# Low parts of streamed weights: from a VectorE subtraction to a ScalarE negation and an adding transfer

## The chip, the cores and the metric

The kernel runs on one core of one Trainium2 chip. The metric is the device time of one launch in microseconds (us). The engines are TensorE (PE, its weight loads shown as PEld), VectorE (DVE), ScalarE (ACT), GpSimd (POOL) and SyncE (SP), which here issues DMA transfers.

## The reference

Two transformer-like networks run one after the other on 512 tokens of width 1024, all in float32. The first is one layer: a modulated norm, one projection `w_in` to queries, keys, values, gates and a recurrent branch, dilated attention in three groups, a gated linear recurrence, and the merge of both branches:

```python
mod = jax.nn.silu(c) @ w_mod + b_mod
h = rms_norm(x, g_pre) * (1 + scale) + shift
q, k, v, g_att, u, g_lru, merge = jnp.split(h @ w_in, split_at, axis=-1)
y_a = (dilated_attention(q, k, v) * jax.nn.silu(g_att)) @ w_pa
y_b = (rg_lru(causal_depthwise_conv(u, conv_w, conv_b), ...) * jax.nn.silu(g_lru)) @ w_pb
out = (gate_a * y_a + gate_b * y_b) @ w_o
x = x + gate * rms_norm(out, g_post)
```

The second is two layers over the 512 tokens and 256 context tokens. Each has four token mixers (a long convolution, differential attention over both streams, spatial gating, a short convolution) that share the projection `w_in_2` (ten parts of 256 columns) and `w_out_2`, and an MLP with a squared relu and 4096 hidden units. The context stream goes through the first layer's mixers and MLP, and in the second layer only through the keys and values.

## The kernel before

Activations lie transposed, 128 channels on the partitions by 512 (or 256) tokens, so a product is a sum over eight such tiles. To keep float32 accuracy with the faster fp32r format, each operand is held as a high part (the value rounded to fp32r) and a low part (the value less its high part), and `mm3` issues three matmuls for each product: high by high (L157), high weight by low activation (L158), low weight by high activation (L159). `tok3` (L164 to L166) does the same with the operands' places exchanged.

Weights stand in DRAM as blocks of 128 x 2048 floats. `whalf` (L141) makes one half of a block, 128 x 1024 or 512 KB: SP loads it into a `raw` buffer (four of them, RAW_BUFS; the load has its priority raised by 4000), ACT copies it to fp32r as `whi` (L149), and DVE subtracts `whi` from `raw` into `wlo` (L150). There are three buffers of `whi` and three of `wlo` (W_BUFS); L149 and L150 have their priority raised by HPS = 400. `whalf` is called 312 times: 8 times for `w_u`, the first projection, and 304 times for all others. `raw_half` with another pool loads the modulation weights (`rawa`), which DVE alone reads (L263); no `whalf` is in that.

`wblock` makes both halves of a block. `gemm` works through a block for its two output tiles and each stream of tokens; for each it passes over half 0 and then half 1, in four k-steps of three matmuls each, into one PSUM tile:

```python
todo = [(mi, st) for mi in range(2) for st in streams]
for grp in ([todo] if together else [[t] for t in todo]):
    pss_ = [ps.g() for _ in grp]
    for h, (hi, lo) in enumerate(halves):
        ...
```

The stages in order: `w_u` (to 66 us), four heads of attention with `w_head`, recurrence and `w_gl` (to about 450 us), the merge with `w_merge`, `w_pb`, `w_pa` (where a block of `w_pa` is loaded for two rounds, so one of its halves is held through the three blocks of the second round) and `w_o`, then for each layer of the second network the input projections (`in`), attention with the short convolution and most of `out_part` between its units, and the MLP (`up`, `down`; layer 0 from 1010 to about 1590 us with part of the context's work at its end, layer 1 from 1807 us). The context's projections of layer 0 (Mixer `mc`) have 256 columns only, and its `out_part("cdab")` holds halves of three blocks at a time.

No order is written out by hand between engines: the program is traced in the order of the source, and when it is built a scheduler fixes each engine's order from priorities and from the times at which it expects operands to be ready. On the chip an engine runs its list strictly in that order and waits where an operand is late. GpSimd's list holds little: 24 `pow` (L225) of the norms, each between a DVE operation and the transposes that spread its result.

Of the kernel before, what the change touches and what calls it, by code (L numbers as in the profile page):

```python
# [10 lines left out]
F32 = mybir.dt.float32  # L11
F32R = mybir.dt.float32r
BF16 = mybir.dt.bfloat16
AF = mybir.ActivationFunctionType
ALU = mybir.AluOpType
# [13 lines left out]
BLOCKS = {}  # L29
# [50 lines left out]
def tile_net(ctx: ExitStack, tc: tile.TileContext, wst, vec, crow, lrow, sgw, cst, xT, xN, cT, out):  # L80
    nc = tc.nc
    V, A, G, T = nc.vector, nc.scalar, nc.gpsimd, nc.tensor
# [3 lines left out]
    def nm(s):  # L86
        uid[0] += 1
        return f"{s}_{uid[0]}"
# [45 lines left out]
    def raw_half(key, h, pool=None):  # L134
        if pool is None:
            t = wpool.tile([P, 1024], F32, tag="raw", name=nm("raw"), bufs=RAW_BUFS)
        else:
            t = pool.tile([P, 1024], F32, tag="rawa", name=nm("rawa"), bufs=rawa_bufs[0])
        with tc.high_priority(offset=HP):
            nc.sync.dma_start(t, wst[BLOCKS[key]][:, h * 1024:(h + 1) * 1024])  # L140
        return t  # L141

    def whalf(key, h, cols):

        hi = wpool.tile([P, 1024], F32R, tag="whi", name=nm("whi"), bufs=W_BUFS)
        lo = wpool.tile([P, 1024], F32R, tag="wlo", name=nm("wlo"), bufs=W_BUFS)
        src = raw_half(key, h)
        with tc.high_priority(offset=HPS):
            A.copy(hi, src)  # L149
            V.tensor_sub(lo, src, hi.bitcast(F32))  # L150
        return hi.rearrange("p (k c) -> p k c", c=cols), lo.rearrange("p (k c) -> p k c", c=cols)

    def wblock(key, kt, cols):
        return [whalf(key, h, cols) for h in range(2)]
# [178 lines left out]
    for m in range(NT):  # L333
        mod_col(m, 1)
        mod_col(m, 0)
        hi, lo = whalf(("w_u", m // 2), m % 2, 1024)
        V.scalar_tensor_tensor(x0[m], x0[m], sc1[:, m:m + 1], pb0 if m else pbp, op0=ALU.mult, op1=ALU.mult)
        A.activation(h1[m][:, 0], x0[m], AF.Identity, bias=sh1[:, m:m + 1])  # L338
        V.scalar_tensor_tensor(h1[m][:, 1], x0[m], sh1[:, m:m + 1], h1[m][:, 0].bitcast(F32),
                               op0=ALU.add, op1=ALU.subtract)  # L340
        for c in range(NT):
            mm3(pu[c], hi[:, 0, c * P:(c + 1) * P], lo[:, 0, c * P:(c + 1) * P], h1[m][:, 0], h1[m][:, 1],
                m == 0, m == NT - 1)
        if m == 3:
            with tc.high_priority(offset=HP):
                nc.sync.dma_start(vecs, vec[:, NV0:NV])
    rawa_bufs[0] = RAWA_BUFS

# [39 lines left out]
    for mp in range(4):  # L388
        u = yap.tile([P, 2, SX], F32, tag="ya", name=nm("u"), bufs=4)
        for i in range(2):  # L390
            m = 2 * mp + i
            dst, src = u[:, i].rearrange("p (i r) -> p r i", r=4), pu[m].rearrange("p (r i) -> p r i", r=4)
# [415 lines left out]
    class Mixer:  # L808
# [334 lines left out]
        def out_part(self, names, done=None, bank=None):  # L1143

            s = self.s
            key = f"out{self.l}"
            for half in range(2):
                w = {n: whalf((key, 2 + half), "ab".index(n), 512) for n in names if n in "ab"}
                for pair in range(2):
                    if "c" in names:  # L1150
                        w["cd"] = whalf((key, half), pair, 256)
                    for i in range(2):
                        p = (bank or ps.g)()[:, :s.n]
                        seq = []
                        if "c" in names:
                            seq += [(w["cd"], kk, i, self.y["cd"[kk // 2], kk % 2]) for kk in range(4)]
                        for n in "ab":
                            if n in names:
                                seq += [(w[n], kk, 2 * pair + i, self.y[n, kk]) for kk in range(2)]
                        for e, ((hi, lo), kk, mi, a) in enumerate(seq):  # L1160
                            c = slice(mi * P, (mi + 1) * P)
                            mm3(p, hi[:, kk, c], lo[:, kk, c], a[:, 0], a[:, 1], e == 0, e == len(seq) - 1)
                        self.add(4 * half + 2 * pair + i, p, done)
# [177 lines left out]


RAW_BUFS = 4
RAWA_BUFS = 4
W_BUFS = 3
ST_BUFS = 2
# [158 lines left out]
```

## Time and profile before

| | us |
|---|---|
| median of 3 runs (lowest, highest) | 2175.99 (2171.11, 2178.37) |
| the profiled execution, its own time | 2175.18 |
| its span from the first to the last instruction | 2173.3 |
| PE busy | 2053.4 |
| DVE busy | 1424.4 |
| ACT busy | 810.1 |
| POOL busy | 27.4 |

Times in the rows are counted from the span's start. A matmul's busy time overlaps the next one's: starts of matmuls, not their durations, tell the pace. The granted clock (PEclk) is 1.00 at 2.4 GHz and 0.50 at 1.2 GHz; its mean over the span is 0.978. A bracket at a row's end is the engine's idle time before it and what ended it.

### The profile page before, as it was taken

What the parts mean: (1) busy time and instruction counts of PE and PEld (TensorE: products, weight loads), DVE (VectorE), ACT (ScalarE), POOL (GpSimd) and SP (SyncE); (2) the same over time, 40 slices, a digit from 0 to 9 for tenths busy, and PEclk for the clock granted to TensorE, in tenths of its full rate; (3) what the DMA queues carried; (4) which work ended last, traced back from release to release, by engine and by line L of the source; (5) the groups of instructions that cost most, each with busy time, mean ns of one, the idle gap of its engine ahead of it and who ended that gap; (6) DMA issues with size and microseconds to landing.
All of it is one profiled execution on the core that took longest, in us unless ns stands there. A gap on an engine that the chain in (4) does not pass through costs nothing.

```text
span 2173.3 us, 28000 instructions
## 1 busy us (share of the span) xinstructions
PE 2053.4 (94%) x11020; PEld 1758.3 (81%) x11020; DVE 1424.4 (66%) x2351; ACT 810.1 (37%) x1266; POOL 27.4 (1%) x28
## 2 busy tenths in 40 slices
PE   7989999999999988998999999999998998999997
PEld 5778788778889777876888888888887787888886
DVE  8778999843458999778354645534798766443444
ACT  3565333432344533645312313123434544232331
POOL 0000000000000000000000000000000000000000
PEclk9999999999999999998999999999999998999998
DMA  8523666523335444222232454422413212333331
GB/s 314 171 92 95 197 222 204 181 94 105 109 111 168 124 121 127 78 78 79 67 127 88 138 169 150 155 67 89 135 59 107 83 59 69 97 97 97 97 97 58
DMA packets 84388, 259.47 MB, mean 119 GB/s; under 512 B 11424, under 2 KB 20256, under 8 KB 84256
## 3 DMA queue, kind: packets, MB, share of 16 engines
q1 hardware_dynamic: 84256, 257.67, 37.6%
q8 instruction: 87, 1.43, 0.3%
q14 instruction: 45, 0.37, 0.1%
HBM read 242.95 MB, written 5.24 MB: 114 GB/s over the span
## 4 chain that ended last, share of the span: by engine, by line
PE 72%; DVE 18%; DMA 3%; issue 3%; ACT 3%; POOL 1%; SPq 0%; POOLq 0%; DVEq 0%; ACTq 0%
PE mm L157 15%; PE mm L159 15%; PE mm L158 15%; PE g L157 5%; PE g L158 5%; PE g L159 5%; DVE wlo L150 3%; DVE ya L872 2%; PE po L1084 2%; DVE rawa L263 2%; DVE j L263 1%; PE sc L1057 1%; DMA rawa<-wst 1%; PE mm L1081 1%; PE mm L208 1%
## 5 line engine op out<-in xcount | busy, mean ns | idle before, releaser
L149 ACT CAST whi<-raw 128x1024 fp32r<-128x1024 f32 x312 | 326.9, 1050 | 536.7 <-PE mm L158 387.4
L150 DVE TENSOR_TENSOR wlo<-raw,whi 128x1024 fp32r<-128x1024 f32 x312 | 380.5, 1222 | 210.7 <-ACT whi L149 205.9
L157 PE MATMUL mm<-h,whi 128*128 128x512 f32 (+1 forms) x992 | 361.0, 366 | 5.7 <-ACT h L338 3.6
L158 PE MATMUL mm<-h,whi 128*128 128x512 f32 (+1 forms) x992 | 361.7, 365 | 0.9 <-DVE h L712 0.9
L159 PE MATMUL mm<-h,wlo 128*128 128x512 f32 (+1 forms) x992 | 361.1, 364 | 0.8 <-DVE wlo L150 0.8
L159 PE MATMUL mm<-hid,wlo 128*128 128x512 f32 (+1 forms) x768 | 272.6, 355 | 1.0 <-DVE wlo L150 1.0
L157 PE MATMUL mm<-hid,whi 128*128 128x512 f32 (+1 forms) x768 | 273.0, 355 | 0.0
L158 PE MATMUL mm<-hid,whi 128*128 128x512 f32 (+1 forms) x768 | 272.8, 355 | 0.0
L157 PEld LDWEIGHTS mm<-h,whi 128*128 128x128 f32 x992 | 188.8, 191 | 37.1 <-ACT h L338 4.0
L158 PEld LDWEIGHTS mm<-h,whi 128*128 128x128 f32 x992 | 188.7, 190 | 31.5 <-DVE h L712 1.9
L157 PE MATMUL g<-h,whi 128*128 128x512 f32 x512 | 205.7, 402 | 8.6 <-DVE v L508 6.0
L159 PEld LDWEIGHTS mm<-h,wlo 128*128 128x128 f32 x992 | 188.6, 190 | 31.2 <-DVE wlo L150 2.0
L158 PE MATMUL g<-h,whi 128*128 128x512 f32 x512 | 204.8, 400 | 0.0
L159 PE MATMUL g<-h,wlo 128*128 128x512 f32 x512 | 204.3, 399 | 0.3 <-DVE wlo L150 0.3
L159 PEld LDWEIGHTS mm<-hid,wlo 128*128 128x128 f32 x768 | 146.1, 190 | 21.5 <-DVE wlo L150 1.4
L157 PEld LDWEIGHTS mm<-hid,whi 128*128 128x128 f32 x768 | 146.4, 191 | 20.2
L158 PEld LDWEIGHTS mm<-hid,whi 128*128 128x128 f32 x768 | 146.3, 191 | 20.0
L1284 DVE SCALAR_TENSOR_TENSOR r<-mm,r 128x512 f32<-128x512 f32 x96 | 57.4, 599 | 114.1 <-ACT r L1283 114.0
L157 PEld LDWEIGHTS g<-h,whi 128*128 128x128 f32 x512 | 98.4, 192 | 26.9 <-issue 6.2
L159 PEld LDWEIGHTS g<-h,wlo 128*128 128x128 f32 x512 | 98.1, 192 | 19.3 <-DVE wlo L150 0.7
L158 PEld LDWEIGHTS g<-h,whi 128*128 128x128 f32 x512 | 98.3, 192 | 17.9
L872 DVE SCALAR_TENSOR_TENSOR ya<-glu,caw,ya 128x512 f32<-128x512 f32 (+1 forms) x180 | 111.6, 656 | 0.5
(309 smaller groups left out, 3462.7 us busy)
## 6 DMA issues: line engine op xcount, KB each, us to landing
raw<-wst SPq DMA_DIRECT2D x312, 512.0 KB, 3.9
rawa<-wst SPq DMA_DIRECT2D x120, 512.0 KB, 4.6
qst<-q SPq DMA_DIRECT2D x48, 64.0 KB, 2.0
kst<-k SPq DMA_DIRECT2D x48, 64.0 KB, 2.0
kst<-k SPq DMA_DIRECT2D x72, 32.0 KB, 2.1
x<-xT SPq DMA_DIRECT2D x4, 512.0 KB, 5.0
hs_d<-c SPq DMA_DIRECT2D x4, 512.0 KB, 2.6
hq<-hs_d SPq DMA_DIRECT2D x4, 512.0 KB, 5.5
```

The source lines that it names most:

```text
L149: A.copy(hi, src)
L150: V.tensor_sub(lo, src, hi.bitcast(F32))
L157: T.matmul(ps, lh, rh, start=start, stop=False)
L158: T.matmul(ps, lh, rl, start=False, stop=False)
L159: T.matmul(ps, ll, rh, start=False, stop=stop)
L208: T.matmul(pt[:, i:i + 1], a[:, i * P:(i + 1) * P], ones1, start=k == 0 and i == 0, stop=k == len(self.parts) - 1 and i == nt - 1, skip_gr ...
L263: V.tensor_tensor_reduce(o, w, row, 0.5, 0.0, ALU.mult, ALU.add, d)
L872: V.scalar_tensor_tensor(self.ya[m], x, w, self.ya[m], op0=ALU.mult, op1=ALU.add)
L1057: T.matmul(st[:, o:e], hd.q[:, w, qt * P:(qt + 1) * P], hd.k[:, w, o - w * nkeys:e - w * nkeys], start=True, stop=True, skip_group_check=True)
L1081: T.transpose(pt[:, i * P:(i + 1) * P], pw[0][:, t0 + i * P:t0 + (i + 1) * P], ident)
L1084: T.matmul(hd.po[:, qt, h % 2], pth[:, i * P:(i + 1) * P], ss.v[:, kt, h], start=i == 0 and qt == 0 and h % 2 == 0, stop=i == nk - 1 and q ...
L1284: V.scalar_tensor_tensor(r, p, 0.0, r, op0=ALU.max, op1=ALU.mult)
```

## The change

For all blocks but `w_u` the subtraction goes. ACT writes the negative of the high part into `wlo`, and a transfer issued by GpSimd adds the raw weights to it from SBUF to SBUF, 512 KB each. The transfer stands under the same raised priority. `raw` is now read by ACT's copy and by the transfer; matmuls on `wlo` wait for the transfer to have landed.

```diff
         with tc.high_priority(offset=HPS):
             A.copy(hi, src)
-            V.tensor_sub(lo, src, hi.bitcast(F32))
+            if key[0] in LO_DMA:
+                A.activation(lo, hi.bitcast(F32), AF.Copy, scale=-1.0)
+                G.dma_start(lo.bitcast(F32), src, accum_op=ALU.add)
+            else:
+                V.tensor_sub(lo, src, hi.bitcast(F32))
@@
 RAW_BUFS = 4
+LO_DMA = tuple({k for k, _ in BLOCKS} - {"w_u"})
```

## Rows read from the trace of the kernel before

**Rows 1.** The page's part 1: busy us, share of the span, instructions.
```profile
PE 2053.4 (94%) x11020; PEld 1758.3 (81%) x11020; DVE 1424.4 (66%) x2351; ACT 810.1 (37%) x1266; POOL 27.4 (1%) x28
```

**Rows 2.** Busy time by stretch: three with a full DVE, and the second MLP.
```profile
core 0: us, PE busy (x) PEld busy (x) DVE busy (x) ACT busy (x) POOL busy (x), PEclk, DMA share, GB/s
163.00:434.70 271.70, 257.57 (x1474) 220.32 (x1473) 251.47 (x475) 103.35 (x170) 0.00 (x0) 0.99 0.56 180
652.00:869.30 217.30, 193.56 (x1264) 175.63 (x1263) 198.62 (x387) 90.81 (x160) 6.62 (x7) 0.95 0.45 135
1575.60:1684.30 108.70, 99.28 (x594) 87.55 (x593) 98.77 (x171) 41.91 (x71) 3.16 (x3) 0.95 0.29 83
...
1820.00:2160.00 340.00, 339.81 (x1504) 281.44 (x1502) 144.66 (x163) 104.89 (x132) 0.00 (x0) 1.00 0.29 89
```

**Rows 3.** PE's waits: line, releaser, us in total, times, longest.
```profile
PE mm L208 <- DVE acc L221: 17.6, 3, 10.4
...
PE g L159 <- DVE wlo L150: 2.4, 4, 0.9
...
PE mm L159 <- DVE wlo L150: 1.7, 4, 1.0
```

**Rows 4.** Timeline (start, us, engine, line, operation) in the second MLP.
```profile
1884.15 1.05 ACT L149 CAST whi<-raw 128x1024 fp32r<-128x1024 f32 x1 [7.11 <-PE mm L158]
...
1885.24 1.23 DVE L150 TENSOR_TENSOR wlo<-raw,whi 128x1024 fp32r<-128x1024 f32 x1 [2.87 <-ACT whi L149]
...
1890.03 0.39 PE L159 MATMUL mm<-hid,wlo 128*128 128x512 f32 x1
```

**Rows 5.** Timeline in the first MLP, both streams.
```profile
1110.32 1.05 ACT L149 CAST whi<-raw 128x1024 fp32r<-128x1024 f32 x1 [11.55 <-PE mm L158]
...
1114.84 0.39 PE L159 MATMUL mm<-hid,wlo 128*128 128x512 f32 x1
```

**Rows 6.** Timeline in the merge, with a half of w_pa held.
```profile
485.71 1.05 ACT L149 CAST whi<-raw 128x1024 fp32r<-128x1024 f32 x1 [1.94 <-PE mm L158]
...
488.89 0.40 PE L159 MATMUL mm<-yb,wlo 128*128 128x512 f32 x1
```

**Rows 7.** Timeline of PE: matmuls of other tiles between a tile's own.
```profile
169.58 0.42 PE L158 MATMUL big<-us,g 128*128 128x512 f32 x1
...
1594.13 0.40 PE L157 MATMUL g<-h,whi 128*128 128x512 f32 x1
1594.36 0.39 PE L158 MATMUL g<-h,whi 128*128 128x512 f32 x1
1594.59 0.28 PE L157 MATMUL g<-hc,whi 128*128 128x256 f32 x1
1594.71 0.40 PE L159 MATMUL g<-h,wlo 128*128 128x512 f32 x1
...
1818.60 0.39 PE L157 MATMUL mm<-h,whi 128*128 128x512 f32 x1
```

**Rows 8.** Groups of instructions: count, busy us, mean ns, idle before and releasers.
```profile
L150 DVE TENSOR_TENSOR wlo<-raw,whi 128x1024 fp32r<-128x1024 f32 x312 | 380.5, 1222 | 210.7 <-ACT whi L149 205.9 <-PE g L159 1.8 <-PE g L158 0.4
...
L149 ACT CAST whi<-raw 128x1024 fp32r<-128x1024 f32 x312 | 326.9, 1050 | 536.7 <-PE mm L158 387.4 <-PE g L158 92.9 <-issue 29.3
...
L225 POOL TENSOR_TENSOR rs<-ms,neghalf 128x4 f32<-128x4 f32 (+2 forms) x24 | 27.1, 1131 | 2135.4 <-DVE ms L233 1832.5 <-DVE ms L1099 161.4 <-DVE ms L929 136.9
```

**Rows 9.** DMA issues: count, KB each, median us from issue to landing.
```profile
raw<-wst SPq DMA_DIRECT2D x312, 512.0 KB, 3.9
...
qst<-q SPq DMA_DIRECT2D x48, 64.0 KB, 2.0
...
hs_d<-c SPq DMA_DIRECT2D x4, 512.0 KB, 2.6
```

**Rows 10.** Timeline of PE in the context's out_part.
```profile
813.95 0.58 PE L159 MATMUL g<-y,wlo 128*128 128x256 f32 x1 [0.90 <-DVE wlo L150]
```

**Rows 11.** A stop of PE, and the stretch behind it (columns as in rows 2).
```profile
858.39 0.55 PE L157 MATMUL mm<-sgs,sv 128*128 128x256 f32 x1 [3.91 <-DVE sb L951]
...
857.90:864.60 6.70, 6.21 (x19) 5.27 (x20) 6.56 (x8) 0.62 (x1) 0.00 (x0) 0.50 0.37 116
```

## The prediction

> **What bounds the kernel now.** I read the page's busy times first [rows 1]: TensorE (PE) is busy 2053.4 of 2173.3 us, so all its idle time is 119.9 us, and nothing done on another engine can give back more. VectorE (DVE) has 1424.4 us, ScalarE (ACT) 810.1, GpSimd (POOL) 27.4. Next the stretches [rows 2]: in the second layer's MLP PE is busy 339.81 of 340 us and DVE less than half, so there PE alone bounds. In the first block's attention, 163 to 435 us, DVE is busy 251.47 of 271.7 us and PE 257.57: DVE is almost as full, but PE stands only 14.1 us. Last the waits of PE [rows 3]: on the low parts of mm3 (L159) it loses 2.4 + 1.7 us in the whole run; the longest in total, 17.6 us, is for a norm's sum of squares, and most of the others are for such chains, which hold no weight work. So the kernel is bound by PE's stream of matmuls, and the weights arrive in time for it. The question is whether they still do.
>
> **How much time a low part has.** A block is two halves; gemm goes over them as half 0, half 1 for its first output tile and again for the second. With W_BUFS = 3 the next block's half 0 is ready early, but its half 1 goes into the buffer that the running block's half 0 leaves late in the block. One such cycle with 512 tokens [rows 4]: the buffer is left and the CAST starts at 1884.15, the subtraction ends at 1886.47, and the first matmul on that low part runs at 1890.03. That is 5.88 us from release to need, 2.3 of them used. In the first layer's MLP, where each block also serves 256 context tokens, the last pass over half 0 is a context pass, so the release comes later: 1110.32 to 1114.84, 4.52 us [rows 5]. While a w_pa half is held one buffer is missing and half 0 itself is late: 485.71 to 488.89, 3.18 us [rows 6]. For blocks with context alone I work it out: matmuls of 256 columns follow each other every 0.12 us [rows 7], a pass over a half has 12, so 1.44 us, and release to need is two passes and two matmuls, 3.1 us.
>
> **The change part by part.** (1) It takes 304 subtractions of 1222 ns off DVE (312 less the 8 of w_u): 371 us [rows 8]. (2) It adds 304 negations to ACT. An ACT pass over 128x1024 is the CAST, 1050 ns [rows 8]; 304 x 1.05 = 319 us, ACT then has 1129 of 2173, no bound, though its evacuations stand up to 1.05 us behind each one; PSUM banks cover that. (3) It adds 304 transfers of 512 KB on GpSimd's queue. In that queue stand the 24 pow of the norms [rows 8]; one may stand behind a transfer that waits for its negation. At one CAST each that is 24 x 1.05 = 25 us at most and nothing at least; I take 5. (4) Raw buffers are left when the transfer has landed instead of after the subtraction. With four of them a load still starts two blocks ahead; I take nothing for it, and name the price of full DMA engines in the first rival.
>
> After the change the chain to a low part is CAST 1.05, negation 1.05, two hops of 0.04 (as between CAST and subtraction [rows 4]), then the transfer, D from issue to landing: 2.18 + D, where it was 2.3. The trace shows no adding transfer and none issued by GpSimd. Its nearest rows [rows 9]: 512 KB out of the SBUF land in 2.6 us (plain, one read), a raw load of the same size takes 3.9, 64 KB take 2.0. From 64 to 512 KB a load costs 1.9 us, so a second read of the whole tile, which an addition needs, about 2.2. The low end of D is 2.6 (the second read hidden), the high end 3.9 + 2.2 = 6.1, and 8.3 if a raw load shares the engines. An estimate from these is 2.6 + 2.2 + an issue of 0.33 = 5.1; I take 5.0, so a chain of 7.2 us.
>
> The Trainium skill says, in "Collectives: The Full Stack", section "The bandwidth ceiling: the fold count and why AG ≠ RS ≠ AR", that an add in a DMA engine runs at half the rate of a copy because it reads two sources. No run here shows that yet. "DMA: Bandwidth & Descriptors", section "Anatomy of one DMA — SWDGE (gpsimd) path", fits a GpSimd transfer as 2.0 us plus bytes over 436 GB/s: 3.2 us for 512 KB; with the read doubled 4.4. Put into the sum below, the first would give about 2221 us (and the third rival's time with a fully adapted order), the second about 2283.
>
> If PE keeps its present order, each block stands for 2.18 + D less the time it has:
> - 60 blocks with 512 tokens outside the attentions (32 in the second MLP, 4 in the first, 12 of the input projections, 12 of the merge and w_o stage): 7.18 - 5.88 = 1.3 us each, 78 us.
> - 29 blocks with both streams (27 in the first MLP, 2 key and value blocks): 7.18 - 4.52 = 2.7, 78 us.
> - 6 blocks with a w_pa half held: 4.0, 24 us.
> - 14 blocks with context alone (10 of in0, 4 of down0): 4.1, 57 us.
> - The context's out_part, which holds all three buffers and already waits for low parts [rows 10]: four changes of weights at D less 0.1, 20 us.
> The w_head, w_gatt, first w_gl, short() and x out_part blocks stand between attention work that PE can do meanwhile: nothing; without that cover 30 blocks would cost 1.3 each, 39 us. Sum 257 us.
>
> But PE's order is made by the build, and the trace shows that it puts other matmuls in where a low part was expected late: at 1594.13 the two L157 and L158 matmuls of g<-h are followed by one of g<-hc, and only then by the L159 that needs the low part. There are 27 places where the instruction after such a pair is not its L159, the first at 169.58 and the last at 1818.60 us [rows 7]. A block taken as half 0, 0, 1, 1 has 10.9 us (one stream), 16.6 (both) or 6.0 (context) from release to need, and 5.9 with a buffer held. Then nothing is left for the first two kinds, 14 x 1.2 = 17 and 6 x 1.3 = 8, with out_part 20: 45 us. How late the build expects an adding transfer no row shows. I take the middle of 45 and 257, 151 us.
>
> What DVE gives back: PE's idle time in the stretches where DVE is over 80% busy is some 47 us (14.1 in 163 to 435, 23.7 in 652 to 869, 9.4 in 1576 to 1684 us [rows 2]). Much of it is chains without a subtraction in them, so I take 20 (bounds 0 and 47). The clock: after the 3.9 us stop at 854 us the granted clock was 0.50 for 6.7 us [rows 11], a loss of some 3.4 us. Of the stops above, 24 are of 4 us and more in the present order; half as long in the middle case, I take 4 falls, 14 us (bounds 0 and 24 x 3.4 = 82).
>
> Sum: +151 - 20 + 14 + 5 = +150 on the profiled execution's 2175.18 us (span 2173.3 and 1.9 around it; the median of the three runs, 2175.99, is 0.8 above): **2325 us**.
>
> **Rivals.** First, slow transfers in the present order: D near 6.5, the order not adapted. Each of the 113 places above then stands 1.5 us longer, 257 + 170 = 427, clock +40, DVE -20: about 2625. For it: the raw loads of the second MLP already take 0.29 of the DMA engines [rows 2], and as many bytes again, read twice, would bring them to about 0.9, where transfers queue. Against it: the order does adapt in the trace. Second, the order adapts fully: 45 - 20 + 5 = +30, 2205 (2185 to 2240). For it: the 27 places. Against it: it must expect at least the D that the chip shows. Third, faster: a D of at most 3.6 fits into the 3.7 us that a 512-token block leaves after the negation, and with an adapted order into the others; then only out_part pays 4 x 3 = 12 and DVE's relief decides: with 30 us of it 2157. The point from which it decides is D = 3.6; plain rows lie on both sides of it (2.6 and 3.9). Fourth, relief and waits cancel, or the low part is hidden everywhere and DVE's relief is worth nothing because PE's stream bounds: 2170 to 2182.
>
> **How the numbers follow.** Forecast (2240 to 2480) 0.50, slow transfers 0.12, full adaptation 0.18, faster 0.13, no change 0.07. Differences within 0.3% (6.5 us) can't be told from none here. So faster 0.13, same 0.07, slower 0.80. The range from 2172 to 2570 leaves out the faster case and the upper end of the slow one. Inside it the forecast's own range is 2240 to 2480.
>
> **What would show it.** Right: waits of PE for DMA on wlo at the head of the half-1 passes of the MLP, 1 to 3 us each, on the order of 100 of them; landing times of the adding transfers of 4.5 to 6 us; DVE near 1055 us and ACT near 1130; DMA share in the second MLP from 0.29 to 0.6 or above. PE busy near 100% in the MLP with L157 and L158 of two tiles alternating would show that the order adapted, and the second or third rival. Landings under 3.6 us would make the prediction wrong on its first term; landings over 6, low by the first rival. A wait of POOL's pow for ACT would show the queue's price; pow rows that begin as soon as now show it at nothing.

## The result, and the profile after

The changed kernel takes 2465.87 us (median of 4 runs, 2462.22 to 2483.36) where the kernel before takes 2175.09 beside it: 1.1354 times as long, with a 95% interval of 1.1296 to 1.1411. The forecast was 2325 us, so the sign was right and the loss of 291 us about twice the 150 forecast. The profiled execution took 2462.22 us, its span is 2460.4, or 287.1 us longer than before; the mean granted clock of PE fell from 0.978 to 0.954. Lines of the gemm stand four lower now: the three matmuls of a low-part product, L157 to L159 before, are L161 to L163, the CAST is still L149, the negation L151, the transfer L152. L169 is `tok3`'s matmul on a low part (L165 before).

From the page of the changed kernel: engines (busy us, share, instructions), queues, the group of the transfers, and landing times (count, KB, median us).

```profile
PE 2133.3 (87%) x11020; PEld 1793.3 (73%) x11020; DVE 1093.0 (44%) x2047; ACT 1103.4 (45%) x1570; POOL 289.1 (12%) x332
...
q0 software_dynamic: 43776, 159.40, 35.8%
...
L152 POOL DMA_DIRECT2D wlo<-raw x304 | 263.5, 867 | 2014.7 <-ACT wlo L151 1786.5
...
raw<-wst SPq DMA_DIRECT2D x312, 512.0 KB, 4.7
...
wlo<-raw POOLq DMA_DIRECT2D x304, 512.0 KB, 5.3
...
qst<-q SPq DMA_DIRECT2D x48, 64.0 KB, 4.1
```

Against [rows 1] DVE is relieved by 331 us and ACT loaded by 293, as meant, and both are under half full. PE does the same 11020 matmuls and is busy 79.9 us longer; its idle time went from 119.9 to 2460.4 - 2133.3 = 327.1 us, 207.2 more. These two make the 287.1. The waits of PE (line, releaser, us in total, times, longest) tell where the second comes from:

```profile
PE mm L163 <- DMA wlo<-raw: 120.3, 81, 4.3
...
PE g L163 <- DMA wlo<-raw: 79.5, 36, 12.2
...
PE mm L245 <- DVE rb L242: 15.0, 10, 2.2
...
PE g L169 <- DMA wlo<-raw: 13.4, 8, 4.1
```

Low parts cost PE 120.3 + 79.5 + 13.4 = 213.2 us, where it was 2.4 + 1.7 in [rows 3] and 0.9 in one wait of L165, 5.0 together: 208.2 more. All other idle time of PE was 114.9 us and is 113.9, so of DVE's 331 us of relief 1 us is left in the sum. (The row for rb is PE's wait for a norm's row, which comes behind GpSimd's pow.)

One cycle of the second MLP in the timeline (start, us, engine, line, operation, in brackets the idle time before and what ended it), to be laid beside [rows 4]:

```profile
2099.75 1.05 ACT L149 CAST whi<-raw 128x1024 fp32r<-128x1024 f32 x1 [0.52 <-PE mm L162]
...
2100.84 1.06 ACT L151 ACTIVATE wlo<-whi 128x1024 fp32r<-128x1024 f32 x1
...
2102.25 0.87 POOL L152 DMA_DIRECT2D wlo<-raw  x1 [8.23 <-ACT wlo L151]
...
2105.22 0.39 PE L161 MATMUL mm<-h,whi 128*128 128x512 f32 x1
...
2105.45 0.39 PE L162 MATMUL mm<-h,whi 128*128 128x512 f32 x1
...
2106.86 0.50 PE L163 MATMUL mm<-h,wlo 128*128 128x512 f32 x1 [1.02 <-DMA wlo<-raw]
```

The buffer comes free at 2099.75 and the low part is used at 2106.86: 7.11 us for the chain, where 5.88 were to be had. Of the 7.11, 4.6 run from the issue of the transfer to its landing, and 0.35 from the end of the negation to the issue. PE stands 1.02 us for it, and its first matmul after the stop takes 0.50 instead of 0.39. By stretch (columns as in rows 2): the attention stage of the first block, a piece around the context's out_part, and the second MLP.

```profile
67.50:510.00 442.50, 376.91 (x1969) 317.22 (x1968) 273.08 (x521) 216.83 (x314) 42.54 (x50) 0.93 0.74 201
...
922.60:984.20 61.60, 32.77 (x203) 29.98 (x203) 18.61 (x34) 17.50 (x20) 6.97 (x8) 0.75 0.75 186
...
2054.20:2445.50 391.30, 359.05 (x1535) 286.88 (x1536) 80.97 (x115) 171.41 (x200) 52.63 (x61) 1.00 0.70 162
```

The same stages in the kernel before, first and third of these:

```profile
66.40:449.20 382.80, 356.25 (x1969) 303.14 (x1968) 324.62 (x574) 168.30 (x263) 0.00 (x0) 0.98 0.50 162
...
1807.90:2158.60 350.70, 350.65 (x1535) 290.04 (x1536) 153.88 (x176) 110.45 (x139) 0.00 (x0) 0.99 0.28 86
```

The second MLP became 40.6 us longer: 32.2 us of idle time and 8.4 of busy time, at a granted clock of 1.00. The attention stage became 59.7 us longer. By the first matmul of each stage in the timelines the whole loss divides like this (us; "present order" is the prediction's sum without an adapted order, divided by stage from its own list):

| stage | present order | after |
|---|---|---|
| w_u, before the first attention | 0 | 1 |
| first block's attention (w_head, w_gatt, w_gl) | 0 | 59.7 |
| merge | 34 | 29.3 |
| w_o | 5 | 3.5 |
| context's in0 and out_part, input projections up to the first MLP | 69 | 61.4 |
| first MLP and the projections up to the second block | 108 | 93 |
| second block's attention | 0 | -1.7 |
| second MLP | 42 | 40.6 |

The last column holds the clock too: the trace has 13 stretches at half clock with 99 us together before, 43 with 227 us after. Half of that is lost at most, 64 us more; counting only the time in which PE is busy there, 68 and 169 us, an estimate is 51. The longest single wait for a low part, 12.2 us, is in the context's out_part: three transfers issued within 1.9 us of each other, from 944.04 us on, land 5.0, 6.8 and 9.7 us after their issue, and PE waits for the last. There the load counts, and not the chain alone.

### The profile page after: what moved, and what is told of

It is laid out like the page before. It is cut to its first block, busy times and chain, and to the rows that moved or that the text cites. A ratio compares the mean times of both kernels' runs of the same rounds, so it can differ in the third digit from the quotient of the medians.

```text
span 2460.4 us, 28758 instructions
## 1 busy us (share of the span) xinstructions
PE 2133.3 (87%) x11020; PEld 1793.3 (73%) x11020; DVE 1093.0 (44%) x2047; ACT 1103.4 (45%) x1570; POOL 289.1 (12%) x332
## 4 chain that ended last, share of the span: by engine, by line
issue 39%; PE 13%; POOL 4%; DMA 3%; DVE 1%; ACT 1%; POOLq 0%; DVEq 0%; ACTq 0%
POOL wlo L152 4%; DMA wlo<-raw 3%; PE g L163 2%; PE g L161 2%; PE g L162 2%; PE po L1088 2%; PE sc L1061 1%; PE mm L163 1%; PE mm L1085 1%; PE mm L161 1%; PE mm L162 1%; POOL rs L229 1%; PE mm L212 0%; PE g L169 0%; DVE sm L1065 0%
## 5 line engine op out<-in xcount | busy, mean ns | idle before, releaser
L149 ACT CAST whi<-raw 128x1024 fp32r<-128x1024 f32 x312 | 326.7, 1048 | 532.8 <-PE mm L162 374.0
L152 POOL DMA_DIRECT2D wlo<-raw x304 | 263.5, 867 | 2014.7 <-ACT wlo L151 1786.5
L163 PE MATMUL mm<-h,wlo 128*128 128x512 f32 (+1 forms) x992 | 368.7, 372 | 63.0 <-DMA wlo<-raw 62.8
L161 PE MATMUL mm<-h,whi 128*128 128x512 f32 (+1 forms) x992 | 364.5, 369 | 5.6 <-ACT h L342 3.6
L162 PE MATMUL mm<-h,whi 128*128 128x512 f32 (+1 forms) x992 | 364.6, 368 | 0.9 <-DVE h L716 0.9
L163 PE MATMUL mm<-hid,wlo 128*128 128x512 f32 (+1 forms) x768 | 280.1, 365 | 50.4 <-DMA wlo<-raw 50.4
L151 ACT ACTIVATE wlo<-whi 128x1024 fp32r<-128x1024 f32 x304 | 320.8, 1056 | 4.6
L161 PE MATMUL mm<-hid,whi 128*128 128x512 f32 (+1 forms) x768 | 276.3, 360 | 0.0
L162 PE MATMUL mm<-hid,whi 128*128 128x512 f32 (+1 forms) x768 | 275.9, 360 | 0.0
L163 PEld LDWEIGHTS mm<-h,wlo 128*128 128x128 f32 x992 | 190.7, 192 | 106.7 <-DMA wlo<-raw 78.1
L163 PE MATMUL g<-h,wlo 128*128 128x512 f32 x512 | 212.4, 415 | 33.1 <-DMA wlo<-raw 33.1
L161 PEld LDWEIGHTS mm<-h,whi 128*128 128x128 f32 x992 | 191.0, 193 | 37.1 <-ACT h L342 4.0
L161 PE MATMUL g<-h,whi 128*128 128x512 f32 x512 | 211.1, 412 | 5.2 <-ACT whi L149 3.2
L162 PEld LDWEIGHTS mm<-h,whi 128*128 128x128 f32 x992 | 190.6, 192 | 33.7 <-DVE h L716 2.2
L162 PE MATMUL g<-h,whi 128*128 128x512 f32 x512 | 210.1, 410 | 0.0
L163 PEld LDWEIGHTS mm<-hid,wlo 128*128 128x128 f32 x768 | 148.9, 194 | 81.4 <-DMA wlo<-raw 61.8
L162 PEld LDWEIGHTS mm<-hid,whi 128*128 128x128 f32 x768 | 149.0, 194 | 21.5
L161 PEld LDWEIGHTS mm<-hid,whi 128*128 128x128 f32 x768 | 149.2, 194 | 20.2
L1302 DVE SCALAR_TENSOR_TENSOR x<-mm,der,x 128x512 f32<-128x512 f32 x64 | 48.0, 751 | 246.6 <-PE mm L163 246.6
L163 PEld LDWEIGHTS g<-h,wlo 128*128 128x128 f32 x512 | 101.1, 198 | 60.0 <-DMA wlo<-raw 41.3
L1287 ACT ACTIVATE r<-mm 128x512 f32<-128x512 f32 x96 | 50.2, 522 | 197.7 <-PE mm L163 197.5
```

The costliest lines, as they stand in the source:

```text
L151: A.activation(lo, hi.bitcast(F32), AF.Copy, scale=-1.0)
L152: G.dma_start(lo.bitcast(F32), src, accum_op=ALU.add)
L161: T.matmul(ps, lh, rh, start=start, stop=False)
L162: T.matmul(ps, lh, rl, start=False, stop=False)
L163: T.matmul(ps, ll, rh, start=False, stop=stop)
L1287: A.activation(r, p, AF.Relu)
```

## The experiments

The theory after the first look was: what costs is the length of the chain CAST, negation, transfer, against the time between the release of a buffer and its use. The rivals: the DMA engines or GpSimd's queue are too full (load); ACT's added pass; the build's changed order of PE.

**The negation without the transfer.** The addition goes back to DVE; ACT's negation stays.

```diff
-                G.dma_start(lo.bitcast(F32), src, accum_op=ALU.add)
+                V.tensor_add(lo, lo.bitcast(F32), src)
```

> The ScalarE half of the change alone: the negation stays, but VectorE adds raw to it, so nothing goes over GpSimd or the DMA engines. Theory (the transfer's latency against the time between a buffer's release and its need is what costs): the chain to a low part is 1.05 + 0.04 + 1.05 + 0.04 + 1.22 = 3.4 us, inside the 5.88 and 4.52 us of most blocks and over only where 3.1 to 3.2 us are there; so 2175 to 2195 us, the second MLP at its 351 us. Rival (ScalarE's 320 us more, and evacuations standing behind the negations, carry much of the 290 us): 2250 us or more, with PE waiting for ScalarE evacuations.

Measured: 2217.27 us, 1.0191 [1.0166, 1.0215]. Its second MLP, and PE's waits for low parts:

```profile
1849.70:2200.70 351.00, 351.00 (x1535) 290.10 (x1536) 152.57 (x176) 171.34 (x200) 0.00 (x0) 0.99 0.28 86
```
```profile
PE mm L163 <- DVE wlo L152: 14.6, 9, 4.0
...
PE g L163 <- DVE wlo L152: 9.8, 6, 3.8
```

The second MLP is as before, 351.0 us, so ACT's load is harmless there. The total lies above what was expected: the chain, one pass of 1.05 us longer than before, is late already in the first MLP and the context's out_part, with 24.4 us of waits in these two rows; PE is also busy 17 us longer, with 20 stretches at half clock instead of 13. Of the 291 us, 42 come with the negation in the chain and 249 with the transfer in place of an addition.

**The transfer beside, nobody waiting for it.** The kernel before with its subtraction, and an adding transfer of 384 KB for each half into one scratch tile that nobody reads.

```diff
             V.tensor_sub(lo, src, hi.bitcast(F32))
+            if key[0] != "w_u":
...
+                G.dma_start(scr[0], src[:, 0:768], accum_op=ALU.add)
```

> The subtraction stays on VectorE; beside it GpSimd issues, for the same 304 halves, an adding transfer of three quarters of the size (384 KB) into a scratch tile that nobody reads. The output is not touched by it. Theory (latency on the path to the low part): with nobody waiting for the transfer the time is near that of before, 2175 to 2205 us, although the DMA engines carry most of the extra bytes. Rival (the DMA engines are too full, or raw buffers come free too late): over 2250 us, with PE waiting for whi or wlo in the MLPs.

Measured: 2285.77 us, 1.0516 [1.0481, 1.0551], nearer to the load rival's number than to the chain's. Second MLP, and waits:

```profile
1931.00:2281.50 350.50, 350.49 (x1535) 289.99 (x1536) 153.87 (x176) 110.42 (x139) 49.33 (x57) 0.99 0.63 150
```
```profile
PE mm L248 <- DVE rb L245: 58.7, 10, 27.2
```
```profile
POOL scr L157 <- DMA scr<-raw: 974.7, 204, 8.7
POOL scr L157 <- DMA raw<-wst: 918.1, 93, 30.1
```

The second MLP loses nothing with 0.63 of the DMA engines busy, so the load costs nothing there. The loss is elsewhere and of another kind: PE waits 58.7 us (up to 27.2 at once) for the norms' row rb, and 29.0 us more for the spatial gating's sv, which hangs on a pow as well. The transfers stand in GpSimd's order behind raw loads, up to 30.1 us, and the norms' pow stands behind them in the same queue. Since all of them add into the one scratch tile, they also follow each other one at a time (the 974.7 us), as the changed kernel's don't. So this run doesn't price the changed kernel's load; it shows what a transfer that waits costs the work behind it on GpSimd. In the changed kernel that cost is absent: PE's waits for rb are 15.0 us there. The attention stage grew by 13.7 us here.

**More time from release to need.** In the changed kernel the gemm takes the output tiles one group at a time over half 0, then over half 1: half 0, 0, 1, 1 instead of 0, 1, 0, 1, which lengthens the time from release to need of a one-stream block from 5.88 us to the 10.9 worked out in the prediction. The same order in the kernel before is the control.

```diff
-            for grp in ([todo] if together else [[t] for t in todo]):
+            for grp in [todo]:
```

> The changed kernel with gemm passing over half 0 for all its output tiles and streams before half 1, in every block. From release to need a block then has 10.9 us (one stream), 16.6 (both) or 6.0 (context) for a chain of 7.2. Theory: the waits for the transfer in both MLPs go; the second MLP falls from 391 to about 352 us and the stretch of the first from 653 to 575-595, the whole to 2310-2360 us; the waits in the merge with a held half, the context's out_part and the attention stage stay in part. Rival (the transfers' throughput bounds, not their latency): the MLPs stay within 10 us of the changed kernel.

> The control: the kernel before, with gemm passing over half 0 for all before half 1. Both theories: the low parts already came in time, so 2165 to 2190 us; any gain in the run of the changed kernel in this order is then not a gain of the order by itself.

Measured: 2327.65 us, 1.0702 [1.0672, 1.0732] with the change; 2178.12, 1.0007 [0.9992, 1.0022] without. The changed kernel gains 138 us, the kernel before nothing. Second MLP and waits of the first of the two:

```profile
1959.70:2310.00 350.30, 350.26 (x1536) 289.37 (x1537) 80.97 (x115) 171.39 (x200) 52.77 (x61) 0.99 0.80 181
```
```profile
PE g L163 <- DMA wlo<-raw: 42.4, 19, 12.0
...
PE mm L163 <- DMA wlo<-raw: 42.0, 19, 8.4
```

The same transfers, over less time and so with a DMA share of 0.80, cost the second MLP nothing once PE comes to a low part 5 us later. That settles this stage for the chain against the load. Over the whole run 90 of the 213 us of waits are left (a third line has 6.0). By stage, the attention still loses 40.9 us (59.7 without this order), the merge and w_o 22.9 (32.8), the context's in0 to the first MLP 54.5 (61.4), and the first MLP with the projections behind it 32.4 (93).

**One stage alone.** The transfers in the second layer's MLP only, and in the first block's attention only.

```diff
-LO_DMA = tuple({k for k, _ in BLOCKS} - {"w_u"})
+LO_DMA = ("up1", "down1")
```
```diff
-LO_DMA = tuple({k for k, _ in BLOCKS} - {"w_u"})
+LO_DMA = ("w_head", "w_gatt", "w_gl")
```

> The change for the 64 halves of the second MLP alone; all other low parts are subtracted on VectorE as before. Theory: each of the 32 blocks stands for the chain of 7.1 us less the 5.88 it has, 1.3 us, so 41 us, all of it between the start of the second MLP and its last matmul (391 us there instead of 351), 2210 to 2222 us in all. Rival (the cost comes from a load on queues and the DMA engines that the whole run builds up): that stretch takes under 375 us.

> The change for w_head, w_gatt and w_gl alone, the weights of the first block's attention stage. The forecast had nothing there; the changed kernel is 61 us later at the stage's end. Theory: this is local, from transfers that share the DMA engines with the modulation weights and from waits for low parts: 50 to 65 us at the start of the merge (w_pb's first matmul at 500 to 514 us instead of 449), and nothing after it, 2225 to 2240 in all. Rival (the loss comes from ScalarE's order or is made good later where VectorE has room): under 2205.

Measured: 2211.66 us, 1.0169 [1.013, 1.0208], with the second MLP at 391.5 us and all before it unchanged (its start lies 1.9 us earlier); and 2238.71 us, 1.0297 [1.0282, 1.0313], with the attention stage 61.9 us longer (59.7 with all transfers). So each of these two stages costs alone what it costs in the whole, and neither is an effect of the other. The second MLP of the first, and some waits of PE and landings in the second:

```profile
1806.00:2197.50 391.50, 359.29 (x1535) 287.02 (x1536) 80.93 (x115) 171.25 (x200) 52.68 (x61) 0.99 0.69 160
```
```profile
PE g L163 <- DMA wlo<-raw: 20.1, 10, 3.5
...
PE big L161 <- DVE sm L545: 19.3, 3, 8.7
...
PE big L161 <- ACT us L195: 12.6, 4, 10.5
...
PE g L169 <- DMA wlo<-raw: 6.4, 3, 3.9
```
```profile
wlo<-raw POOLq DMA_DIRECT2D x48, 512.0 KB, 6.5
```

In the attention PE waits for low parts 26.5 us, and also for attention work of DVE and ACT, in few long waits. The transfers land in 6.5 us here, in a stage whose loads take 0.50 of the DMA engines in the kernel before; with the transfers the share is 0.74 in the changed kernel. The share alone doesn't set the landing time: in w_o it is 0.80, and the landings there take 4.8 us.

**A shorter chain, first try.** The negation reads the raw half and no longer the CAST's result, so that it and the transfer can go ahead of the CAST; once alone, once with the halves in turn.

```diff
-            A.copy(hi, src)
             if key[0] in LO_DMA:
-                A.activation(lo, hi.bitcast(F32), AF.Copy, scale=-1.0)
+                A.activation(lo, src, AF.Copy, scale=-1.0)
                 G.dma_start(lo.bitcast(F32), src, accum_op=ALU.add)
+            A.copy(hi, src)
```

> The changed kernel with the negation made straight from raw, ahead of the high part's CAST, so the chain to a low part is one ScalarE pass (1.05 us) shorter, 6.1 instead of 7.1 us, with the same transfers. Theory (latency): the second MLP stands 0.2 us in a block instead of 1.3 and falls from 391 to about 358 us; the whole by 70 to 110 us, to 2355 to 2395. Rival (throughput of the transfers or ScalarE's load, both unchanged): within 15 us of the changed kernel's 2466.

> Both mitigations: negation first, and half 0 for all before half 1. Theory (latency): the MLPs have no waits for the transfer, and the merge, the context's projections and out_part lose one pass per wait, so 2260 to 2305 us against 2328 with the order alone. Rival (what is left at 2328 is not latency but DMA load and ScalarE's order): 2315 or more.

Measured: 2471.18 us, 1.136 [1.1329, 1.1391], and 2326.27, 1.0695 [1.0661, 1.0728]: no different from the changed kernel and from the halves in turn. The timeline of the first, in the second MLP, says why:

```profile
2108.31 1.06 ACT L152 CAST whi<-raw 128x1024 fp32r<-128x1024 f32 x1 [0.46 <-PE mm L162]
...
2109.26 1.05 ACT L150 ACTIVATE wlo<-raw 128x1024 fp32r<-128x1024 f32 x1
...
2110.67 0.86 POOL L151 DMA_DIRECT2D wlo<-raw  x1 [9.91 <-ACT wlo L150]
...
2115.26 0.50 PE L163 MATMUL mm<-h,wlo 128*128 128x512 f32 x1 [0.88 <-DMA wlo<-raw]
```

The CAST still stands first. It waits for whi's buffer, which L162 releases, one matmul ahead of the L163 that releases wlo's; so it is ready before the negation, and the build put it first (the next try, which takes this difference away, turns the order round). The edit didn't do what it says, so both expectations are missed without telling anything of the chain.

**A shorter chain, second try.** As before, with high and low part in one tile, so that both are released together.

```diff
-        hi = wpool.tile([P, 1024], F32R, tag="whi", name=nm("whi"), bufs=W_BUFS)
-        lo = wpool.tile([P, 1024], F32R, tag="wlo", name=nm("wlo"), bufs=W_BUFS)
+        both = wpool.tile([P, 2, 1024], F32R, tag="whl", name=nm("whl"), bufs=W_BUFS)
+        hi, lo = both[:, 0], both[:, 1]
```

> High and low part in one tile, so that both come free with the block's last matmul on the half, and the negation from raw really stands ahead of the CAST (with two tiles it did not: the high part's buffer comes free one matmul earlier, and ScalarE's list kept the CAST first). The chain to a low part is then one pass shorter, less the 0.23 us by which its buffer comes free later. Theory (latency): in the second MLP a block stands 0.4 us instead of 1.3, that stretch 391 to about 364 us or less; the whole 30 to 100 us below the changed kernel, 2365 to 2435. Rival (throughput of transfers, ScalarE's load): within 15 us of 2466, the second MLP still 391.

Measured: 2422.3 us, 1.1134 [1.1092, 1.1177], in the range expected. Timeline and second MLP:

```profile
2061.63 1.06 ACT L150 ACTIVATE whl<-raw 128x1024 fp32r<-128x1024 f32 x1 [0.46 <-PE mm L163]
...
2062.60 1.03 ACT L152 CAST whl<-raw 128x1024 fp32r<-128x1024 f32 x1
...
2063.18 0.86 POOL L151 DMA_DIRECT2D whl<-raw  x1 [6.29 <-ACT whl L150]
...
2068.28 0.50 PE L163 MATMUL mm<-h,whl 128*128 128x512 f32 x1 [0.80 <-DMA whl<-raw]
```
```profile
2040.70:2407.10 366.40, 358.79 (x1536) 286.68 (x1536) 80.86 (x115) 167.83 (x200) 52.70 (x61) 1.00 0.73 170
```

Now the negation goes first, and the transfer is issued 1.55 us after ACT's start where it was 2.50. The second MLP loses 15.7 us over its 32 blocks instead of 40.6: 0.78 us less for each, for 0.95 us less of chain and a buffer that comes free 0.23 us later. PE's waits there fall from 32.2 to 6.9 us in 25 waits, of which the row above shows the longest; the rest of the 15.7 is busy time. So the loss follows the chain's length.

**A smaller transfer.** Columns 0 to 511 are subtracted on DVE, only 512 to 1023 are negated and sent, 256 KB each.

```diff
-                A.activation(lo, hi.bitcast(F32), AF.Copy, scale=-1.0)
-                G.dma_start(lo.bitcast(F32), src, accum_op=ALU.add)
+                V.tensor_sub(lo[:, 0:512], src[:, 0:512], hi[:, 0:512].bitcast(F32))
+                A.activation(lo[:, 512:1024], hi[:, 512:1024].bitcast(F32), AF.Copy, scale=-1.0)
+                G.dma_start(lo[:, 512:1024].bitcast(F32), src[:, 512:1024], accum_op=ALU.add)
```

> Only columns 512 to 1023 of a half take ScalarE's negation and the transfer, now 256 KB; columns 0 to 511 are subtracted on VectorE. Those columns are needed two k-steps (1.36 us with 512 tokens) later and the transfer is half as long. Theory (latency): landing falls from 5.3 to 3.5-4.5 us, no wait in the second MLP (350 to 355 us there), the whole 2200 to 2290. Rival (each transfer costs a fixed price, whatever its size or the time it is needed): 2400 or more.

Measured: 2278.53 us, 1.049 [1.0462, 1.0519], as expected. Second MLP and landing:

```profile
1910.80:2260.90 350.10, 350.02 (x1535) 289.11 (x1536) 121.52 (x176) 147.03 (x200) 52.71 (x61) 1.00 0.57 132
```
```profile
wlo<-raw POOLq DMA_DIRECT2D x304, 256.0 KB, 3.9
```

With a landing of 3.9 us and half a negation the chain fits into the 5.88 us, and the second MLP has no loss. The edit does two things at once: it shortens the chain, and the columns that wait for it are needed two k-steps later. The attention stage still loses 35.3 us.

**No low part at all.** The kernel before without the subtractions; the high part stands in as low part, so that PE does the same matmuls.

```diff
...
-            V.tensor_sub(lo, src, hi.bitcast(F32))
+            if key[0] == "w_u":
+                V.tensor_sub(lo, src, hi.bitcast(F32))
+            else:
+                lo = hi
```

> The kernel before with the low parts of all weights but w_u's left out: the third matmul of each product is still issued, on the high part. VectorE so loses its 304 subtractions and nothing takes their place; the output lacks these terms. It bounds from above what freeing VectorE can give. Theory (PE's stream and chains without subtractions bound): 2150 to 2172 us, 0 to 25 below before. Rival (VectorE bounds the attention stages, and the change's cost hides a real gain): 2130 us or less.

Measured: 2137.16 us, 0.9814 [0.9788, 0.984], between the range of the theory and that of the rival. Its page:

```profile
PE 2045.5 (96%) x11020; PEld 1752.0 (82%) x11020; DVE 1087.1 (51%) x2047; ACT 807.5 (38%) x1266; POOL 26.2 (1%) x28
```

This is what there is to gain if low parts cost nothing anywhere: 38.5 us of span, of which 3.1 up to the end of the attention stage, 12.1 from there to the end of the context's in0, 10.4 from there to the first MLP, and 12.9 behind its start. As far as the build's order stays like this, it bounds what any way of taking the subtraction off DVE can bring, and it holds the waits for low parts (5.0 us) as well as DVE's time. PE's idle time that isn't for low parts is 2134.8 - 2045.5 = 89.3 us here, 25.6 less than the 114.9 before. None of the other kernels was faster than the kernel before.

## Why the prediction was half right

What held:

- The bound. PE's stream is what sets the time, and most of the loss is waits of PE for low parts: 81 + 36 + 8 = 125 of them with 213.2 us. In the MLPs, where the prediction named some 100 of 1 to 3 us, there are 63, and 54 of them have that length.
- The chain. D was taken at 5.0 us, between 2.6 and 6.1; the median is 5.3 (4.5 to 10.2). The 7.2 us of the chain are 7.11 in the timeline above: the landing there is shorter than the 5.0 taken, and the hop to the issue longer than 0.04. The price of a block of 512 tokens, 1.3 us, is 40.6 / 32 = 1.27 in the second MLP; that it fits so well is partly luck, since 1.01 of it is the wait and 0.26 is busy time, which the prediction didn't have. The halves in turn, the one tile and the smaller transfer each moved this stage as that reading says; the control shows that the order alone is worth nothing. This holds for that stage; in the attention the cause is mixed (below).
- The engines. DVE 1093 us (1055 forecast; the run without any low part has 1087, since a subtraction's time partly overlaps its neighbour's), ACT 1103 (1130), DMA share of the second MLP 0.70 (0.6 or above).

What failed, step by step. The forecast's span was 2173.3 + 150 = 2323.3 us, 137 short. The measured time still lies inside the forecast's own range, 2240 to 2480 us, near its upper end; it does so by the width of that range.

- *"I take the middle of 45 and 257, 151 us"*: the order adapted less than halfway. Outside the attention PE waits 185 us for low parts, between the 257 of the present order and the 45 of the adapted one. In the first MLP 26 blocks have a fill of most or all of one context pass, as this piece of PE's timeline of the changed kernel shows:

```profile
1202.71 0.39 PE L161 MATMUL mm<-h,whi 128*128 128x512 f32 x1
1202.94 0.39 PE L162 MATMUL mm<-h,whi 128*128 128x512 f32 x1
1203.17 0.28 PE L161 MATMUL mm<-h,whi 128*128 128x256 f32 x1
...
1204.48 0.28 PE L163 MATMUL mm<-h,wlo 128*128 128x256 f32 x1
...
1206.12 0.50 PE L163 MATMUL mm<-h,wlo 128*128 128x512 f32 x1 [1.36 <-DMA wlo<-raw]
```

  A context pass of 1.44 us goes ahead of the low part, and PE still stands 1.36 us, where 2.7 were counted for such a block. Blocks with one stream got next to none: in the second MLP, L161 and L162 are followed by the wait, as in the cycle shown above; in the merge there are fills of some ten matmuls at two places. The 27 places of [rows 7] were read as a sign that the build can fill a gap of any length; the fill shown there is a single matmul of 256 columns. Outside the attention the stages lost 228 us, against 151 taken: 77 of the 137. Of these, 34 are waits (185 less 151), and 43 are what DVE's relief leaves of 59 us in which PE is busy longer, at half clock or with slow first matmuls after a stop; for the clock the forecast has a term of its own. A longer fill was to be had: the halves in turn give 138 us back.
- *The attention stage at nothing*: the cover that the prediction named wasn't enough. The stage lost 59.7 us, more than the 39 named for the case without cover. Alone it loses 61.9, so it is this stage's own transfers that do it. By the windows above PE is busy 20.7 us longer there, with the granted clock at 0.93 instead of 0.98, and idle 65.6 us instead of 26.6. Of that idle time 28.5 us are for low parts; waits on attention work of DVE and ACT rose from 25 to 37 us. In the timeline of the changed kernel DVE stands for the loads of a mask (mt) and of the rows of L267 (rawa), and PE for DVE:

```profile
81.41 0.23 DVE L439 CAST mask<-mt 128x128 bf16<-128x128 f32 x1 [8.79 <-DMA mt<-cst]
...
238.86 1.23 DVE L267 CUSTOM_DVE_ANT_0 j<-rawa,c2row 128x1024 bf16<-128x1024 f32 x1 [6.05 <-DMA rawa<-wst]
...
243.07 0.77 PE L161 MATMUL big<-qk,qk 128*128 128x512 f32 x1 [8.50 <-DVE sm L545]
```

  Two of these waits are behind late loads: the 8.50 us above, and 10.2 us at 83.06, for an operation of ACT that has itself stood 10.81 us for a load of gate weights (gm). That load took from 70.89 to 81.85 us; in the kernel before it took from 69.58 to 74.90. Here the prediction's part (4), raw buffers that are left later, "I take nothing for it", bears on the matter, and nothing in the runs tests it. SP issues all loads in one list, and in this stage it stands twice as long for a raw buffer to come free (first row before, the other two after), while DVE's waits for the modulation weights that stand in the same list grow from 1.7 us to 35:

```profile
SPq L140 <- DVE wlo L150: 114.2, 39, 9.7
```
```profile
SPq L140 <- DMA wlo<-raw: 229.9, 48, 19.1
```
```profile
DVE j L267 <- DMA rawa<-wst: 27.7, 14, 6.0
```

  These loads also land later once issued (6.2 us instead of 4.6), so which of the two holds DVE up is open. For the weights themselves the term was rightly nothing: PE waits 5.8 us for high parts in the whole run, 1.5 before. How much of the rest is due to loads that land late, and how much of the clock's part to which wait, isn't settled. With the negation alone the stage loses 1.8 us, with transfers beside 13.7, with half-size transfers 35.3, with the halves in turn 40.9, with the shorter chain 55.2. So ACT's pass is not it. Half the bytes help more here than 0.95 us less of chain, but they shorten the landing as well, so the two causes stay mixed.
- *DVE's relief at 20 us* shows as 1 us: the idle time of PE that isn't for low parts went from 114.9 to 113.9. By itself the relief was sized about right, since the run without any low part has 25.6 us less of that idle time. In the changed kernel it fell by 12 us outside the first attention, and inside it the new waits, 11 us more, take that back. Where a full DVE was read as the cause, in that attention, there was little to gain: without any low part the stage is only 4.0 us shorter, though DVE is busy 324.62 of its 382.80 us before.
- *The clock at 14 us* was about 51, and 64 at most: 43 stretches at half clock and not 13. That lies inside the bounds of 0 and 82 in the prediction; the term was mis-sized with the first two steps.
- *The queue's 5 us* for pow behind transfers were nothing: PE's waits for rb are 15.0 us after and 16.0 before, and each of the 24 pow begins within 0.16 us of the end of the DVE operation before it in both kernels. The price is real, though, where a transfer itself waits long: 58.7 us for rb with the scratch tile.

Terms together: 77 + 59 + 20 - 14 - 5 = 137. (59 is the attention with `w_u` and the second block's attention; the relief is added and the clock and queue terms are taken off since the stages hold all three.)

A fourth pair of weight buffers, which would let the CAST start earlier, wasn't tried, and neither was a fifth raw buffer.

## What to carry to other kernels

Before an operation is handed from an engine to a transfer, lay the latency of its whole chain beside the time from the release of the buffer to the first use, for each kind of block: a step that takes 1.2 us on an engine and 5.3 as a transfer is free only where that time allows it, however idle the engines are. If the time is short, look for the order of the consumer that lengthens it first, and price the order as it stands, not one that the build might find. And a nearly full engine beside the bounding one is worth what the bounding one waits for it, which a run without that work shows at once: here at most 38.5 us, against 371 us of work taken away.

## What the runs showed of the hardware

- The adding transfer from SBUF to SBUF lands in 5.3 us for 512 KB and 3.9 us for 256 KB (medians of 304), and in 6.5 us in the attention stage alone. From the first two, an estimate: 1.4 us for each 256 KB, or some 187 GB/s, and 2.5 us besides. The shortest landings, 4.48 and 3.24 us, give 1.24 us for each 256 KB, or some 211 GB/s, and 2.0 us besides. The Trainium skill's rule, told there of collectives in "Collectives: The Full Stack", section "The bandwidth ceiling: the fold count and why AG ≠ RS ≠ AR", that an add runs at half the rate of a copy, agrees with the slope of the shortest if a copy runs at the 436 GB/s that "DMA: Bandwidth & Descriptors", section "Anatomy of one DMA — SWDGE (gpsimd) path", gives; the 3.2 us of that page's fit for 512 KB are not met, while the prediction's 4.4 with the read doubled come close to the shortest landing.
- GpSimd is busy 867 ns with the issue of each such transfer, 263.5 us in all, and about as long (52.71 us for 61 instructions in the second MLP) where a transfer has 256 KB.
- Other loads suffer: raw halves land in 4.7 us instead of 3.9, the 64 KB loads of q in 4.1 instead of 2.0 [rows 9].
- Stops of 1 us in each 12 us of the second MLP left the granted clock at 1.00, though the first matmul after each took 0.50 us instead of 0.39. The stretch around the context's out_part, with PE busy 32.77 of 61.60 us, ran at 0.75.
